# Sample tokens' y from the old states: four units' column-part products issued together

## The chip, the cores and the metric

One core of a Trainium2 chip runs the kernel in one launch. The metric is device time in microseconds (us), the median of the runs. TensorE (PE) multiplies and transposes, VectorE (DVE), ScalarE (ACT) and GpSimd (POOL) do the element work, SyncE (SP) issues the transfers.

## What is computed

The reference is one inference step of a hybrid decoder layer: a half-step SwiGLU FFN, a token mixer with a pooling branch and a Mamba-2 (SSD) branch, and a second half-step FFN. 1024 prompt tokens and 64 sample tokens (8 sequences of 8) go through it in float32. What matters here is the SSD branch of the sample tokens, which starts from given states:

```python
D_INNER = 2048; SSD_HEAD_DIM = 64; N_SSD_HEADS = 32; N_SSD_GROUPS = 4; D_STATE = 128
# state_ssm (1, 8 sequences, 32 heads, 64, 128) is h0 of the sample tokens
# exact per-token recurrence h_t = exp(dt_t A) h_{t-1} + dt_t x_t B_t^T, y_t = h_t C_t
def step(h, inp):
    s_c, d_c = inp
    return h * d_c[..., None, None] + s_c, h
h_last, h_prev = lax.scan(step, h0..., (st, chunk_decay))
y_off = jnp.einsum('bclgn,bcgrpn,bclgr->bclgrp', cr, h_prev, jnp.exp(a_cs))
y = y_diag + y_off
```

For the sample tokens there is one chunk, so `h_prev` is the old state h0: `y_off` is C times h0 times a decay, and the new state is h0 times a decay plus a sum over the eight new tokens.

## The kernel before

Activations lie with channels on the partitions, in two halves of tokens: 512 prompt tokens, then 512 prompt and the 64 sample tokens (576, in two pieces of 288). A dense projection of a 128-channel tile is a series of matmuls 128 x 128 x 288 in three products (high and low parts); `pz`, `pc` and `pso` are the PSUM tiles of such projections. Their weights come in pairs `wh`, `wl` by transfers on SP's queue, some tiles ahead.

Around this main stream run generators, called chains, which emit the small steps. `tick()` is called between the k steps of a projection; a chain's next step is emitted once an estimate `pe[0]` of PE time has passed its due time, which is the time before its last step plus what it yielded. `STEP_S` is 2.5. A scheduler then orders each engine's instructions; PE, ACT, DVE and SP each run theirs in that order.

`ssd_group` is the chain of one of four head groups. It ends, in the second half, with the sample tokens: `ssd_b` with `c == 4`. Their states are worked on in eight units, `(pr, bh)`: a pair of heads `pr` out of four, for four sequences `bh` out of two fours. A unit is one tile of 128 x 4 x 128: (head, channel) by sequence by state. For each unit the code does this:

- `load` (L1183): a transfer of the old states into `h0` (in the profile the tile is `h`), two units ahead.
- `turn` (L1188): four transposes into PSUM `ph0T`, copied by ACT into `h0T` (L1193). Before the change this is done one unit ahead.
- pyos (L1211, the helper's line is L161): for each of the four sequences, 32 columns of C against the turned state, into 32 partitions of the PSUM tile `po`, called `pyos`. Each product uses a 32-column part of the array. It is float32, two instructions each, so eight for a unit.
- pnew (L1214): one product of 96 rows by 512 columns, the new tokens' share of the state.
- DVE (L1216) forms the new state in place, and SP stores it (L1219).
- Behind the fourth pair: ACT copies `po` into `yt` (L1222), PE turns it back (`pyT`), and DVE multiplies it by the decay (L1228).

The other half of the sample tokens' y comes from `pyd` (L1237), in 64-column parts; `pfin` turns the prompt's last state. In group 0 the sample stage comes at the end of the projection `pz`, and its steps run into the next group's `pc`; in groups 1 to 3 it runs beside `pz`.

Of the kernel before, what the change touches and what calls it, by code (L numbers as in the profile page):

```python
# [14 lines left out]
P = 128  # L15
# [47 lines left out]
def tile_hybrid_pool_ssd_macaron(  # L63
# [19 lines left out]
    def nm(s):  # L83
        uid[0] += 1
        return f"{s}_{uid[0]}"

    def act(shape=(P, 576), dt=F32, name="a"):
        return sp.tile(list(shape), dt, tag="act", bufs=N_ACT, name=nm(name))
# [22 lines left out]
    def psum(tag="ps", name="ps"):  # L111
        npd = stage["npd"]
        return stage["ps"].tile([P, 512], F32, tag=tag, bufs=npd if tag == "pd" else 8 - npd, name=nm(name))
# [46 lines left out]
    def mm(out, lhsT, rhs, start=True, stop=True, free=False):  # L160
        T.matmul(out, lhsT, rhs, start=start, stop=stop, skip_group_check=free)  # L161
        pe[0] += max(out.free_size(), 64) / 2400.0 * (1 if rhs.dtype == F32R else 4)

    def tr(out, in_, idn):
        T.transpose(out, in_, idn)  # L165
        pe[0] += 0.107
# [1000 lines left out]
    def ssd_b(h, g, c, a, hold, Cf, y4, dts):  # L1167

        dt, acs, dtd, cd, cdp = dts
        abs_, xp, xd, ea, btok, L, tok = a  # L1170
        smp = c == 4
        hc = c * NH + g * HPG
        hcs = slice(hc, hc + HPG)
        ysl = y4[:, :, tok]
        first = h == 0 and c == 0
        if smp:
            units = [(pr, bh) for bh in range(2) for pr in range(4)]

            def src(u):
                gp = g * 4 + u[0]  # L1180
                return state_ssm[0, u[1] * 4 : u[1] * 4 + 4, 2 * gp : 2 * gp + 2].rearrange("b h p n -> (h p) b n")

            def load(u):  # L1183
                t = act((P, 4, P), name="h0")
                dma(t, src(u))
                return t

            def turn(h0):  # L1188
                pt = psum("ps", "ph0T")
                for b in range(4):  # L1190
                    tr(pt[:, b * P : (b + 1) * P], h0[:, b, :], ident)
                hT = act((P, 4, P), name="h0T")
                S.copy(hT.rearrange("p b n -> p (b n)"), pt)  # L1193
                return hT

            h0s = {0: load(units[0]), 1: load(units[1])}
            yield STEP_S
            hTs = {0: turn(h0s[0])}
            for i, (pr, bh) in enumerate(units):
                if i + 2 < len(units):  # L1200
                    h0s[i + 2] = load(units[i + 2])
                yield STEP_S
                if i + 1 < len(units):
                    hTs[i + 1] = turn(h0s[i + 1])
                hT, h0 = hTs.pop(i), h0s.pop(i)
                gp = g * 4 + pr


                if pr == 0:
                    po = psum("ps", "pyos")  # L1210
                for b in range(4):  # L1211
                    mm(po[b * 32 : (b + 1) * 32, pr * P : (pr + 1) * P], Cf[:, 512 + bh * 32 : 544 + bh * 32], hT[:, b, :])
                pn = psum("ps", "pnew")
                mm(pn, xd[bh][0][:, pr * P : (pr + 1) * P], xd[bh][1].rearrange("p b n -> p (b n)"))  # L1214
                for b in range(4):
                    V.scalar_tensor_tensor(h0[:, b, :], h0[:, b, :], cdp[0][:, gp, bh * 4 + b : bh * 4 + b + 1],  # L1216
                                           pn[:, b * P : (b + 1) * P], op0=ALU.mult, op1=ALU.add)
                dst = new_ssm_s[0, bh * 4 : bh * 4 + 4, 2 * gp : 2 * gp + 2].rearrange("b h p n -> (h p) b n")
                dma(dst, h0)  # L1219
                if pr == 3:  # L1220
                    yt = act((P, 512), name="yt")
                    S.copy(yt, po)  # L1222
                    pt = psum("ps", "pyT")
                    for k in range(4):
                        tr(pt[:, k * P : (k + 1) * P], yt[:, k * P : (k + 1) * P], ident)
                    own = bass.AP(pt.tensor, pt.offset, [list(pt.ap[0]), [P, 4], [40, 4], [1, NT]])
                    e = ea[:, :, bh * 32 : (bh + 1) * 32].rearrange("p q (b t) -> p q b t", t=NT)
                    V.tensor_tensor(e, own, e, op=ALU.mult)  # L1228
        elif not first:
            po = psum("ps", "pyo")  # L1230
            for pr in range(4):
                mm(po[:, pr * L : (pr + 1) * L], hold[:, pr * P : (pr + 1) * P], Cf[:, tok])
        py = psum("ps", "pyd")
        for i in range(HPG):
            m_ = abs_[i // abs_[0].shape[1]][:L, i % abs_[0].shape[1], :]
            hh = slice((i % 2) * HD, (i % 2 + 1) * HD)
            mm(py[hh, (i // 2) * L : (i // 2 + 1) * L], xp[:L, i * HD : (i + 1) * HD], m_)  # L1237
        pyv = py[:, : 4 * L].rearrange("p (q l) -> p q l", l=L)
        if first:
            V.tensor_tensor(ysl, ysl, pyv, op=ALU.add)  # L1240
        else:
            if not smp:
                V.tensor_tensor(ea, po.rearrange("p (q l) -> p q l", l=L), ea, op=ALU.mult)
            V.tensor_tensor(ea, ea, pyv, op=ALU.add)
            V.tensor_tensor(ysl, ysl, ea, op=ALU.add)
# [22 lines left out]
    def ssd_group(h, g, Bf, Cf, xs4, y4, dts):  # L1268
# [6 lines left out]
        for c in range(4 + h):  # L1275
            ga = ssd_a(h, g, c, Bf, Cf, xs4, dts)
            next(ga)
            yield step
            try:
                next(ga)  # L1280
            except StopIteration as e:
                a = e.value
            yield step
            if prev:
                for w in ssd_b(h, g, *prev, Cf, y4, dts):
                    yield w
            prev = (c, a, ssd_st(h, g, c, a, dts))
        yield step
        for w in ssd_b(h, g, *prev, Cf, y4, dts):
            yield w  # L1290
# [266 lines left out]
```

## Time and profile before

| | |
|---|---|
| time, median of 3 runs | 2952.33 us (2952.29 to 2953.47) |
| span of the profiled execution | 2950.3 us |
| instructions in the profile | 52088 |
| PE busy | 2900.3 us, 98% of the span |
| DVE / ACT / POOL busy | 1646.5 / 1187.0 / 445.1 us |
| pyos matmul instructions | 256, median 285 ns, from 1708.6 to 2056.6 us |
| ph0T transposes | 128, median 272 ns |
| pnew matmuls | 32, median 499 ns |

The span runs from the first to the last instruction of the execution that the profiler recorded; the profile gives no other time for that execution, and the times of the runs lie about 2 us above the span. [...]

### The profile page before, as it was taken

What the parts mean: (1) busy time and instruction counts of PE and PEld (TensorE: products, weight loads), DVE (VectorE), ACT (ScalarE), POOL (GpSimd) and SP (SyncE); (2) the same over time, 40 slices, a digit from 0 to 9 for tenths busy, and PEclk for the clock granted to TensorE, in tenths of its full rate; (3) what the DMA queues carried; (4) which work ended last, traced back from release to release, by engine and by line L of the source; (5) the groups of instructions that cost most, each with busy time, mean ns of one, the idle gap of its engine ahead of it and who ended that gap; (6) DMA issues with size and microseconds to landing.
All of it is one profiled execution on the core that took longest, in us unless ns stands there. A gap on an engine that the chain in (4) does not pass through costs nothing. (4 is left out here: it accounts for less than half of the span.)

```text
span 2950.3 us, 52088 instructions
## 1 busy us (share of the span) xinstructions
PE 2900.3 (98%) x19740; PEld 2689.1 (91%) x19740; DVE 1646.5 (56%) x3134; ACT 1187.0 (40%) x2418; POOL 445.1 (15%) x528
## 2 busy tenths in 40 slices
PE   7999999999999999999999999999999999999998
PEld 6999999789988888788999988999999999997898
DVE  5654445434273897777633776867665443443432
ACT  5444444333242665443332454442333433342322
POOL 5433333000000000000000010100034333330000
PEclk9999999999999999999999999999999999999999
DMA  4465554864335888678434566556574522236652
GB/s 131 155 220 176 164 161 152 271 201 142 101 98 168 276 258 265 196 225 286 118 97 152 170 184 183 168 155 186 178 240 155 165 90 76 79 106 203 197 179 72
DMA packets 542273, 501.36 MB, mean 170 GB/s; under 512 B 36388, under 2 KB 391780, under 8 KB 542014
## 3 DMA queue, kind: packets, MB, share of 16 engines
q1 hardware_dynamic: 542006, 498.03, 54.0%
q8 instruction: 155, 2.54, 0.4%
q14 instruction: 96, 0.79, 0.1%
q10 hardware_dynamic: 16, 0.00, 0.0%
HBM read 355.94 MB, written 142.20 MB: 169 GB/s over the span
## 5 line engine op out<-in xcount | busy, mean ns | idle before, releaser
L290 DVE TENSOR_TENSOR wl<-wraw,wh 128x512 fp32r<-128x512 f32 (+1 forms) x416 | 282.8, 681 | 394.7 <-ACT wh L289 386.6
L289 ACT ACTIVATE wh<-wraw 128x512 fp32r<-128x512 f32 (+1 forms) x416 | 256.4, 617 | 603.0 <-PE po L161 233.7
L161 PE MATMUL pw<-hi,wh 128*128 128x288 f32 (+1 forms) x1248 | 361.3, 289 | 2.6 <-DVE t L560 2.2
L161 PE MATMUL pw<-hi,wl 128*128 128x288 f32 (+1 forms) x1248 | 360.1, 289 | 0.0
L161 PE MATMUL pw<-lo,wh 128*128 128x288 f32 (+1 forms) x1248 | 359.9, 288 | 0.0
L161 PE MATMUL pw<-X,wh 128*128 128x288 f32 (+1 forms) x1872 | 356.9, 289 | 0.2 <-ACT t L556 0.2
L161 PEld LDWEIGHTS pw<-X,wh 128*128 128x128 f32 x1872 | 295.8, 190 | 0.4 <-ACT t L556 0.4
L161 PE MATMUL po<-hh,wh 128*128 128x288 f32 (+1 forms) x1056 | 288.1, 330 | 6.8 <-ACT hh L350 6.6
L161 PE MATMUL po<-hr,wh 128*128 128x288 f32 (+1 forms) x1056 | 289.4, 328 | 0.0
L161 PE MATMUL po<-hh,wl 128*128 128x288 f32 (+1 forms) x1056 | 288.6, 328 | 0.0
L161 PE MATMUL pw<-X,wl 128*128 128x288 f32 (+1 forms) x936 | 270.1, 289 | 0.0
L161 PEld LDWEIGHTS pw<-hi,wh 128*128 128x128 f32 x1248 | 236.2, 189 | 3.5 <-DVE t L560 2.6
L161 PEld LDWEIGHTS pw<-lo,wh 128*128 128x128 f32 x1248 | 236.1, 189 | 0.0
L161 PEld LDWEIGHTS pw<-hi,wl 128*128 128x128 f32 x1248 | 236.1, 189 | 0.0
L456 DVE TENSOR_TENSOR wl<-s,wh 128x512 fp32r<-128x512 f32 x168 | 123.4, 736 | 145.3 <-ACT wh L455 142.2
L161 PEld LDWEIGHTS po<-hh,wh 128*128 128x128 f32 x1056 | 179.0, 189 | 24.3 <-ACT hh L350 11.1
L161 PEld LDWEIGHTS po<-hr,wh 128*128 128x128 f32 x1056 | 179.9, 189 | 15.8 <-DVE hr L352 2.3
L161 PEld LDWEIGHTS po<-hh,wl 128*128 128x128 f32 x1056 | 180.0, 189 | 14.2 <-DMA wl<-part 0.4
L161 PEld LDWEIGHTS pw<-X,wl 128*128 128x128 f32 x936 | 178.1, 190 | 0.0
L455 ACT ACTIVATE wh<-s 128x512 fp32r<-128x512 f32 x168 | 106.2, 632 | 174.4 <-PE pw L161 170.7
L161 PE MATMUL pc<-hi,wh 128*128 128x288 f32 (+1 forms) x576 | 161.5, 334 | 0.0
L161 PE MATMUL pc<-lo,wh 128*128 128x288 f32 (+1 forms) x576 | 158.2, 328 | 0.0
(341 smaller groups left out, 6391.0 us busy)
## 6 DMA issues: line engine op xcount, KB each, us to landing
wh<-part SPq DMA_DIRECT2D x204, 256.0 KB
wl<-part SPq DMA_DIRECT2D x204, 256.0 KB
wraw<-in_ffn_w_in_dram SPq DMA_DIRECT2D x188, 256.0 KB
wraw<-in_w_in_dram SPq DMA_DIRECT2D x180, 256.0 KB
wraw<-in_ffn_w_out_dram SPq DMA_DIRECT2D x120, 256.0 KB
part<-wh SPq DMA_DIRECT2D x112, 256.0 KB
part<-wl SPq DMA_DIRECT2D x112, 256.0 KB
ab<-acsd SPq DMA_DIRECT2D x64, 256.0 KB
```

Of the source, the lines that this page charges most:

```text
L161: T.matmul(out, lhsT, rhs, start=start, stop=stop, skip_group_check=free)
L289: S.activation(wh, raw, AF.Copy)
L290: V.tensor_tensor(wl, raw, wh.bitcast(F32), op=ALU.subtract)
L455: S.activation(wh, a, AF.Copy)
L456: V.tensor_tensor(wl, a, wh.bitcast(F32), op=ALU.subtract)
```

## The change

The products of pyos leave their units. The turned states of four units are kept, and behind the fourth unit's pnew the sixteen products of all four are issued in a row into one PSUM tile, which is allocated only there. A unit's transposes are issued in the unit's own step, not one unit ahead. A yield of 1.0 is put between the copy of `po` and its transposes.

```diff
             h0s = {0: load(units[0]), 1: load(units[1])}
+            hTs = {}
             yield STEP_S
-            hTs = {0: turn(h0s[0])}
             for i, (pr, bh) in enumerate(units):
                 if i + 2 < len(units):
                     h0s[i + 2] = load(units[i + 2])
+                hTs[pr], h0 = turn(h0s[i]), h0s.pop(i)
                 yield STEP_S
-                if i + 1 < len(units):
-                    hTs[i + 1] = turn(h0s[i + 1])
-                hT, h0 = hTs.pop(i), h0s.pop(i)
                 gp = g * 4 + pr
-                if pr == 0:
-                    po = psum("ps", "pyos")
-                for b in range(4):
-                    mm(po[b * 32 : (b + 1) * 32, pr * P : (pr + 1) * P], Cf[:, 512 + bh * 32 : 544 + bh * 32], hT[:, b, :])
                 pn = psum("ps", "pnew")
                 mm(pn, xd[bh][0][:, pr * P : (pr + 1) * P], xd[bh][1].rearrange("p b n -> p (b n)"))
...
                 if pr == 3:
+                    po = psum("ps", "pyos")
+                    for q in range(4):
+                        for b in range(4):
+                            mm(po[b * 32 : (b + 1) * 32, q * P : (q + 1) * P], Cf[:, 512 + bh * 32 : 544 + bh * 32], hTs[q][:, b, :])
+                    hTs = {}
                     yt = act((P, 512), name="yt")
                     S.copy(yt, po)
+                    yield 1.0
                     pt = psum("ps", "pyT")
```

On PE, in head group 1, a unit stands like this before the change (each row is an instruction or a number of equal ones; the names are PSUM tile, moving or stationary operand, with their buffers' numbers):

```order
L161 MATMUL pz_20235<-hi_15086,wl_20276 128x288
L161 MATMUL pz_20236<-hi_15086,wl_20276 128x288
L165 MATMUL ph0T_20290<-ident,h_4164_20224 128x128 x4
L161 MATMUL pyos_20297<-h0T_20264,Cf_17828 32x128 x4
L161 MATMUL pnew_20302<-bblk_20098,X_4140_20091 128x512
L161 MATMUL pz_20235<-hi_15113,wh_20274 128x288
```

Twelve rows of pz follow, and the next unit. After the change the same unit stands as follows, in the same place:

```order
L161 MATMUL pz_20235<-hi_15086,wl_20276 128x288
L161 MATMUL pz_20236<-hi_15086,wl_20276 128x288
L161 MATMUL pnew_20290<-bblk_20098,X_4140_20091 128x512
L165 MATMUL ph0T_20299<-ident,h_4164_20224 128x128 x4
L161 MATMUL pz_20235<-hi_15113,wh_20274 128x288
```

The unit has lost pyos, pnew stands ahead of the next unit's transposes, and eighteen rows of pz follow. Behind the fourth unit of that group the order after the change has the products of all four:

```order
L161 MATMUL pz_20324<-hi_15113,wl_20387 128x288
L161 MATMUL pnew_20407<-bblk_20098,X_4140_20091 128x512
L161 MATMUL pyos_20414<-h0T_20266,Cf_17828 32x128 x4
L161 MATMUL pyos_20414<-h0T_20304,Cf_17828 32x128 x4
L161 MATMUL pyos_20414<-h0T_20349,Cf_17828 32x128 x4
L161 MATMUL pyos_20414<-h0T_20383,Cf_17828 32x128 x4
L161 MATMUL pz_20323<-hi_15135,wh_20385 128x288
```

Six rows of pz lie between this run and the transposes `pyT` of its result. Groups 2 and 3 and the second batch of group 0 have the same form. In the first batch of group 0, PE's rows after the change are these, behind the first two units and fourteen rows of pc:

```order
L165 MATMUL ph0T_18936<-ident,h_3924_18902 128x128 x4
L161 MATMUL pnew_18943<-bblk_18766,X_3901_18759 128x512
L165 MATMUL ph0T_18952<-ident,h_3928_18918 128x128 x4
L161 MATMUL pnew_18959<-bblk_18766,X_3901_18759 128x512
L161 MATMUL pyos_18966<-h0T_18909,Cf_17335 32x128 x4
L161 MATMUL pyos_18966<-h0T_18925,Cf_17335 32x128 x4
L161 MATMUL pyos_18966<-h0T_18941,Cf_17335 32x128 x4
L161 MATMUL pc_19114<-lo_15016,wh_19116 128x288
```

Three more rows of pc and then the fourth unit's pyos follow, so this batch is in two pieces. Outside the sample stages the order of PE differs from before only in a few places behind group 0, where `pyo`, `pyd` and some transposes of the next group's chunks stand some rows later.

## The prediction

> **What bounds the kernel now.** I read the page first, then busy time by stretches around the four places where the edited code runs, then TensorE's waits there, then the timeline inside them. The page:
>
> ```profile
> span 2950.3 us, 52088 instructions
> ...
> PE 2900.3 (98%) x19740; PEld 2689.1 (91%) x19740; DVE 1646.5 (56%) x3134; ACT 1187.0 (40%) x2418; POOL 445.1 (15%) x528
> ...
> PEclk9999999999999999999999999999999999999999
> ```
>
> TensorE (PE) is busy 98% of the span at its full granted clock; no other engine passes 56%. The busy time by stretches, one row for each of the four sample stages and, second, the stretch behind the first of them (columns: stretch, its length, then busy time of PE, PEld, DVE, ACT and POOL):
>
> ```profile
> 1707.00:1726.00 19.00, 18.44 (x181) 14.46 (x180) 10.29 (x36) 6.28 (x12) 0.19 (x1) 1.00 0.81 237
> 1726.00:1745.00 19.00, 18.32 (x136) 17.23 (x136) 15.99 (x37) 11.32 (x25) 4.96 (x10) 1.00 0.62 181
> ...
> 1812.00:1836.00 24.00, 24.00 (x225) 20.47 (x224) 11.95 (x41) 6.97 (x14) 0.19 (x1) 1.00 0.79 230
> ...
> 1930.00:1956.00 26.00, 25.85 (x227) 22.36 (x226) 11.10 (x36) 7.25 (x15) 0.00 (x0) 1.00 0.72 214
> ...
> 2036.00:2060.00 24.00, 24.00 (x225) 20.48 (x224) 12.77 (x43) 6.33 (x12) 0.00 (x0) 1.00 0.79 228
> ```
>
> Three sample stages have next to no idle PE, the first (head group 0) half a microsecond. So the time that counts is how long each instruction holds PE's in-order stream, from its start to the next start: the ends are modelled and overlap. All waits of PE from 1700 to 2100 us:
>
> ```profile
> PE pso L161 <- ACT craw L817: 1.2, 1, 1.2
> PE ph0T L165 <- DMA h<-in_state_ssm_dram: 0.7, 2, 0.5
> PE prb L161 <- POOL rsm L358: 0.7, 1, 0.7
> ```
>
> No weight load is waited for here, though the state loads and stores share SP's queue with them. One unit of group 1, from PE's timeline (start, length, instruction):
>
> ```profile
> 1818.37 0.43 PE L161 MATMUL pz<-hi,wl 128*128 128x288 f32 x2
> 1818.64 0.60 PE L165 MATMUL ph0T<-ident,h 128*128 128x128 f32 x4
> 1819.17 0.43 PE L161 MATMUL pyos<-h0T,Cf 128*32 128x128 f32 x8
> 1819.53 0.50 PE L161 MATMUL pnew<-bblk,X 96*128 96x512 f32 x1
> 1819.87 0.43 PE L161 MATMUL pz<-hi,wh 128*128 128x288 f32 x2
> ...
> 1821.46 0.60 PE L165 MATMUL ph0T<-ident,h 128*128 128x128 f32 x4
> ```
>
> The unit's own rows hold PE from 1818.64 to 1819.87, 1.23 us: four transposes 0.53, the four pyos products (two instructions each) 0.36, pnew 0.34. Twelve pz follow in 1.59, so 0.1325 each. The length of a pyos instruction hides that the eight start nearly together:
>
> ```profile
> L161 PE MATMUL pyos<-h0T,Cf x256: 272/285/298, 1708.6 to 2056.6; 128*32 128x128 f32 x128
> ```
>
> With the row's 0.43 and an instruction of 0.27 to 0.30, all eight start within about 0.15 of each other, and pnew starts some 0.2 after the last of them. That 0.2 repeats in every unit.
>
> **What a pyos group costs.** Group 0 also has places without one, and one where it stands alone between pc products:
>
> ```profile
> 1711.01 0.60 PE L165 MATMUL ph0T<-ident,h 128*128 128x128 f32 x4
> 1711.37 0.48 PE L161 MATMUL pnew<-bblk,X 96*128 96x512 f32 x1
> 1711.68 0.29 PE L161 MATMUL pc<-hi,wl 128*128 128x288 f32 x1
> ...
> 1712.52 0.52 PE L165 MATMUL ph0T<-ident,h 128*128 128x128 f32 x3 [0.54 <-DMA h<-in_state_ssm_dram]
> ...
> 1713.77 0.43 PE L161 MATMUL pc<-hi,wh 128*128 128x288 f32 x2
> 1714.13 0.42 PE L161 MATMUL pyos<-h0T,Cf 128*32 128x128 f32 x8
> 1714.49 0.53 PE L161 MATMUL pc<-lo,wh 128*128 128x288 f32 x2
> 1714.86 0.42 PE L161 MATMUL pc<-hi,wl 128*128 128x288 f32 x2
> ```
>
> Transposes and pnew without pyos between them hold PE 0.67 (1711.01 to 1711.68) against 1.23: pyos costs 0.56. Alone: 1713.77 to 1714.86 is 1.09 for four pc (4 x 0.1325 = 0.53) and the group, again 0.56. About 0.2 of it is streaming; the rest is entering the narrow shape, running dry behind it, and a late first instruction after it (pc x2 takes 0.37 there, not 0.265).
>
> **What a further group in the same run costs.** No two pyos groups are neighbours before the change. The nearest row is pyd, which uses 64-column parts, two at a time, and reuses each part eight times:
>
> ```profile
> 1702.13 1.09 PE L161 MATMUL pyd<-ab,xdt 128*64 128x128 f32 x16
> 1703.16 0.54 PE L161 MATMUL pz<-hi,wh 128*128 128x288 f32 x2
> ```
>
> and the durations of these sixteen (shortest, median, longest, ns):
>
> ```profile
> L161 PE MATMUL pyd<-ab,xdt x16: 272/272/324, 1702.1 to 1703.0; 128*64 128x128 f32 x16
> ```
>
> The last of 16 starts at 1702.13 + 1.09 - 0.27 = 1702.95; that is seven steps from pair to pair, 0.117 each, with no stop where a part gets new weights. A pyos group is two fours, so I take 2 x 0.117 = 0.23 for each further group. Bounds: 0.22, if the first step of pyd is the long one, and 0.36, if each group runs dry before the next (the pyos row itself). I take the pyd end: same 128 rows, same 128 moving columns, same mixture of reuse.
>
> The weight loads of pyos are not much shorter than that step:
>
> ```profile
> L161 PEld LDWEIGHTS pyos<-h0T,Cf x256: 106/108/110, 1708.6 to 2056.4; 128*32 128x32 f32 x128
> ```
>
> [...]
>
> **The sum.** Before, 32 groups stand in 32 runs (four head groups, eight units). After, they stand in nine: the order puts four together in seven batches, and three and one in the first batch of group 0. Joined groups: 32 - 9 = 23. Saved: 23 x (0.56 - 0.23) = 7.6 us. All of it lies on PE, which is the bound, so it counts in full. The transposes, pnew, pz, pc and all copies keep their number; DVE, ACT and POOL do the same work.
>
> Moved pieces, each with its cover:
>
> - pnew now comes out of the pz stream ahead of the transposes. Two in a row show its price:
>
> ```profile
> 1722.61 0.71 PE L161 MATMUL pnew<-bblk,X 96*128 96x512 f32 x2
> 1723.15 0.42 PE L161 MATMUL pc<-hi,wl 128*128 128x288 f32 x2
> ```
>
> 0.27 each, the late first instruction after the transposes included; in the sum it is within the 0.67 pair. I take no extra; bounds -0.04 a unit (0.27 against the 0.31 of pnew in the pair), 1.3 in all, and, as a rival, +0.41 a unit.
>
> - The first batch of group 0. The third and fourth transposes wait for state loads issued at 1707.56 to 1708.54. Before, the fourth set starts at 1712.52, where 1711.68 + 0.13 was possible: 0.7 lost. After, PE reaches it by 1707.26 (first transposes) + two pairs 1.34 + 14 pc 1.86 + one pair 0.67 = 1711.1, so it waits 1.4 for the same landing. Price +0.7; bounds 0 (an earlier landing) and +1.0.
>
> ```profile
> 1707.26 1.03 PE L165 MATMUL ph0T<-ident,h 128*128 128x128 f32 x8
> 1707.56 0.98 SPq L1185 DMA_DIRECT2D h<-in_state_ssm_dram x2
> ```
>
> - The later state loads come two units ahead of their transposes, not one, so the other 0.2 of that wait (group 2) goes: -0.2.
> - The first pyos of the fourth unit waits for the last copy of its batch by ACT:
>
> ```profile
> 1819.28 0.59 ACT L1193 COPY h0T<-ph0T 128x512 f32<-128x512 f32 x1 [1.62 <-PE ph0T L165]
> ```
>
> This copy ends 1.23 after its transposes begin. A late one would hold everything behind pyos on PE; 18 pz (2.4 us) lie between, in group 0 pnew and older groups. The wait for yt ahead of pyT has six pz or pc, 0.8 us, as cover; if ACT is late there, some tenths in eight places, at most +0.8 in all. I take zero.
> - SP: state stores wait for DVE and stand between weight loads; the unit takes 18 pz in place of 12, so the queue is less dense. Zero, since no weight load is waited for now.
> - Behind group 0 the 1.2 wait of pso for the craw copy sits in a DVE-heavy stretch, where the order puts pyo and pyd later. PE arrives earlier by group 0's share, about one microsecond. Bounds: the wait goes (-1.2) or eats that share (+1.0). Zero taken.
>
> Total: -7.6 + 0.7 - 0.2 = -7.1 us. Against the profiled execution that is a span of 2943.2. The median of the runs is 2952.33, 2.0 above the span (what lies around it, unchanged): 2945.2.
>
> **Rivals.**
>
> 1. *Each group runs dry before the next one in a run.* Then a further group costs 0.36: 23 x 0.20 = 4.6, less the 0.5 net of the other terms: 2948.2. For: before, nothing follows a pyos group within 0.2. Against: pyd.
> 2. *Weights come late for each four.* A four then takes a step and a load of the row above: 2 x (0.117 + 0.108) = 0.45, saved 23 x 0.11 = 2.5, less 0.5: 2950.3. For: the loads of pyos and its products share one stream of four parts. Against: pyd again. [...]
>
> 3. *Group 0's gain is lost behind it*, with a longer craw wait and late yt copies: 7.1 - 1.0 - 0.8 = 5.3 saved: 2947.0. For: that stretch has PE waiting for ACT and DVE already. Against: the order also moves DVE work out of its way.
> 4. *Slower: pnew's 96 rows drain the array when entered from a full stream.* Before, pnew always stands behind transposes, a pyos group or another pnew, where a drain could be hidden. If entering and leaving it cost what they do for pyos, 0.56 less its 0.15 of starts = 0.41, times 32 is 13.1: 6.0 slower, 2958.3. It decides from 0.22 a unit. Against: transposes to pnew show no gap (1711.01 to 1711.37 for four), and two pnew take 0.54.
>
> That the grouping does not happen is no rival: the order shows it, apart from the one batch split in three and one.
>
> **Chances.** The forecast's case 0.75, rivals 0.09, 0.04, 0.05 and 0.07. About 0.2% (5.9 us) is what a measurement can tell from no change, so faster means below 2946.4. Of the forecast's 0.75 I put 0.04 above that line, since 7.1 has only 1.2 to spare against waits that I set to zero: faster 0.71; same 0.04 + 0.18 = 0.22; slower 0.07. The range reaches down to 2943.1 (steps of 0.11: 23 x 0.34 = 7.8; the craw wait gone, 1.2; group 2's 0.2; no price in group 0: 9.2 saved; pnew's 1.3 is not added, as that many ends seldom meet) and up to 2948.4, past rivals 3 and 1.
>
> **What would show it.** In the changed profile a run of 32 pyos instructions should hold PE 0.56 + 3 x 0.23 = 1.25, seven times; rows of pnew and ph0T in the stream together 0.67; PE's busy time should fall by about 7 us; the wait of ph0T for its state load should be one of about 1.4 less what the modelled ends hide. A run of 1.6 means rival 1, near 1.9 rival 2; pnew followed by a gap means rival 4. The prediction is wrong if the runs take 1.25 and the time still does not fall: then PE's new slack went into waits on ACT or DVE behind group 0.

## The result

The changed kernel takes 2941.63 us (median, 2940.19 to 2943.37) against 2952.31 (2948.60 to 2953.47) for the kernel before in the same comparison, six runs each: a ratio of 0.9969 on record, 95% interval 0.9959 to 0.9979 (it is not the quotient of the two medians, which is 0.9964). It is faster by more than 0.2%, as forecast; the median lies 1.5 us below the low end of the predicted range (2943.1, which is 0.9969 of the 2952.33 that the prediction started from). In two further comparisons, beside 26 runs each of the kernel before, the difference was 8.4 and 8.0 us (2942.00 against 2950.36, ratio 0.9975 [0.9966, 0.9984]; 2942.14 against 2950.15, ratio 0.9972 [0.9962, 0.9981]). Predicted were 7.1.

The head of the page of the changed kernel:

```profile
span 2939.7 us, 52093 instructions
...
PE 2891.4 (98%) x19740; PEld 2688.6 (91%) x19740; DVE 1644.6 (56%) x3134; ACT 1186.9 (40%) x2418; POOL 445.3 (15%) x528
```

The span fell by 10.6 us and PE's busy time by 8.9; no other engine moved by more than 2. The end of the first batch of group 1, from PE's timeline, and a unit of it:

```profile
1810.67 0.40 PE L161 MATMUL pnew<-bblk,X 96*128 96x512 f32 x1
1810.90 0.60 PE L165 MATMUL ph0T<-ident,h 128*128 128x128 f32 x4
1811.26 0.50 PE L161 MATMUL pz<-hi,wh 128*128 128x288 f32 x2
1811.60 0.42 PE L161 MATMUL pz<-lo,wh 128*128 128x288 f32 x2
...
1819.83 0.40 PE L161 MATMUL pnew<-bblk,X 96*128 96x512 f32 x1
1820.16 1.08 PE L161 MATMUL pyos<-h0T,Cf 128*32 128x128 f32 x32
1821.17 0.53 PE L161 MATMUL pz<-hi,wh 128*128 128x288 f32 x2
1821.54 0.43 PE L161 MATMUL pz<-lo,wh 128*128 128x288 f32 x2
```

The 32 pyos hold PE from 1820.16 to 1821.17, 1.01. Around them, pnew's step is 0.33 and not 0.23, and the next two pz take 0.37 and not 0.265 (two of the prediction's 0.1325): 0.10 and 0.105 more. Together 1.22; predicted 1.25. pnew and the transposes without pyos hold 0.23 + 0.36, and the late pz behind them 0.08: 0.67, as predicted. There is no gap behind pnew, so rival 4 is out.

**Where the time went.** One product, `pcb` with 64 columns, is issued once at the start of each group's sample work, and `pss` on 64 rows ends the part behind group 3. Their starts cut the program into stretches. Before, from PE's timeline (start, length, instruction):

```profile
1695.65 0.33 PE L161 MATMUL pcb<-Cf,Bf 128*64 128x64 f32 x2
1795.96 0.33 PE L161 MATMUL pcb<-Cf,Bf 128*64 128x64 f32 x2
1918.66 0.33 PE L161 MATMUL pcb<-Cf,Bf 128*64 128x64 f32 x2
2019.86 0.33 PE L161 MATMUL pcb<-Cf,Bf 128*64 128x64 f32 x2
2087.56 0.43 PE L161 MATMUL pss<-ident,rsm 64*128 64x64 f32 x2
```

and in the changed kernel:

```profile
1696.14 0.33 PE L161 MATMUL pcb<-Cf,Bf 128*64 128x64 f32 x2
1793.83 0.33 PE L161 MATMUL pcb<-Cf,Bf 128*64 128x64 f32 x2
1914.20 0.33 PE L161 MATMUL pcb<-Cf,Bf 128*64 128x64 f32 x2
2013.00 0.33 PE L161 MATMUL pcb<-Cf,Bf 128*64 128x64 f32 x2
2079.28 0.43 PE L161 MATMUL pss<-ident,rsm 64*128 64x64 f32 x2
```

The distances between these rows, and from the last one to the end of the span, for every execution profiled in this study (us; the kernels are those of the experiments below):

| kernel | joins | group 0 | group 1 | group 2 | group 3 | behind |
|---|---|---|---|---|---|---|
| before | 0 | 100.31 | 122.70 | 101.20 | 67.70 | 862.74 |
| before, again | 0 | 100.17 | 123.15 | 101.06 | 67.95 | 861.72 |
| changed | 23 | 97.69 | 120.37 | 98.80 | 66.28 | 860.42 |
| changed, again | 23 | 98.84 | 120.37 | 98.80 | 66.26 | 859.81 |
| changed, third | 23 | 99.05 | 120.37 | 98.79 | 65.58 | 859.95 |
| apart | 0 | 99.40 | 122.42 | 100.80 | 68.30 | 860.23 |
| pairs | 12 | 98.07 | 120.97 | 99.40 | 66.87 | 859.93 |
| eight | 28 | 99.50 | 120.08 | 98.51 | 65.90 | 860.13 |
| eight, again | 28 | 99.56 | 120.09 | 98.51 | 65.98 | 858.81 |
| ahead | 24 | 99.84 | 120.44 | 98.87 | 66.33 | 860.85 |
| twice | 23 | 100.36 | 122.12 | 100.54 | 68.06 | 860.03 |
| group 0 old | 18 | 100.09 | 120.38 | 98.80 | 66.30 | 860.68 |
| group 0 only | 5 | 97.63 | 122.56 | 101.12 | 68.46 | 859.90 |

From before to changed, group 0 gives 2.62, group 1 2.33, group 2 2.40, group 3 1.42: 8.77 in the edited part. Another 2.32 lies behind it, where the edit changes nothing, and 0.49 is lost ahead of it. The table is the instrument of all that follows: in groups 1 and 2 it repeats to 0.01 between executions of the changed kernel. Each row is one execution, and a wait that another lacks shows in full. In "before, again" group 1 is 0.45 longer, by a wait of PE for a state load:

```profile
1827.42 0.63 PE L165 MATMUL ph0T<-ident,h 128*128 128x128 f32 x4 [0.47 <-DMA h<-in_state_ssm_dram]
```

The first profile of before has none there, but 0.15 of it in group 2. Without these two waits the stretches of groups 1 and 2 agree to 0.02.

### The profile page after: what moved, and what is told of

The parts are those of the page before. It is cut to its first block, busy times and chain, and to the rows that moved or that the text cites. A ratio compares the mean times of both kernels' runs of the same rounds, so it can differ in the third digit from the quotient of the medians.

```text
span 2939.7 us, 52093 instructions
## 1 busy us (share of the span) xinstructions
PE 2891.4 (98%) x19740; PEld 2688.6 (91%) x19740; DVE 1644.6 (56%) x3134; ACT 1186.9 (40%) x2418; POOL 445.3 (15%) x528
## 4 chain that ended last, share of the span: by engine, by line
PE 93%; DMA 2%; DVE 2%; ACT 1%; issue 1%; SPq 0%; POOL 0%; POOLq 0%; ACTq 0%; DVEq 0%
PE pw L161 28%; PE po L161 17%; PE pc L161 9%; PE pg L161 8%; PE pz L161 7%; PE pso L161 5%; PE pu L161 5%; PE pwo L161 3%; PE pbp L161 3%; DMA hr<-hd 1%; PE pyd L161 1%; PE pst L161 1%; PE pyo L161 1%; PE pgm L161 1%; PE ptx L161 0%
## 5 line engine op out<-in xcount | busy, mean ns | idle before, releaser
L161 PEld LDWEIGHTS po<-hh,wh 128*128 128x128 f32 x1056 | 178.8, 188 | 23.9 <-ACT hh L350 10.6
L161 PE MATMUL pc<-hi,wl 128*128 128x288 f32 (+1 forms) x576 | 158.2, 328 | 0.0
```

## Experiments

**Theories.** *Joins*: a pyos group costs 0.56 alone and 0.23 as a further one of a run, so each join gives 0.33. Rivals: each group still runs dry (0.20 a join), or the weights come late (0.11 a join), and the rest of the gain comes from the transposes and pnew having moved, or from the part behind group 0. Every edit below is against the changed kernel.

**The moves without the joins (apart).** Transposes in the unit's own step, as in the changed kernel; the products of each unit stay by themselves.

```diff
                 gp = g * 4 + pr
+                if pr == 0:
+                    po = psum("ps", "pyos")
+                for b in range(4):
+                    mm(po[b * 32 : (b + 1) * 32, pr * P : (pr + 1) * P], Cf[:, 512 + bh * 32 : 544 + bh * 32], hTs[pr][:, b, :])
                 pn = psum("ps", "pnew")
...
                 if pr == 3:
-                    po = psum("ps", "pyos")
-                    for q in range(4):
-                        for b in range(4):
-                            mm(po[b * 32 : (b + 1) * 32, q * P : (q + 1) * P], Cf[:, 512 + bh * 32 : 544 + bh * 32], hTs[q][:, b, :])
-                    hTs = {}
```

> Undoes the grouping alone: the transposes stay in the unit's own step as after the change, but each unit's four products are issued in the unit again, so pyos stands in 32 runs. Theory (joined groups save 0.34 us each, since a run of four holds PE 1.22 us with its edges and four single groups 4 x 0.56): no join, so the time is that of before, 2951 to 2953 us. Rival (the gain comes from moving the transposes and the state loads' lead): 2941 to 2943 us, as after the change.

Measured: 2947.05 us (2944.50 to 2949.88) against 2951.07, ratio 0.9989 [0.9981, 0.9998]. This is 4.0 less than before, more than the theory had. By the table: 0.91 in group 0, 0.28 in group 1, 0.40 in group 2, 0.6 more in group 3, and 2.5 less behind the edited part. Most of the miss is not from the edited code's own rows. What is: 0.28 and 0.40, of which the gone state wait is 0.15 in group 2. The prediction's bound of -0.04 a unit for the moved pnew would be 0.3 a group; it had been left at zero. In PE's timeline of this kernel, a unit reads:

```profile
1814.33 0.42 PE L161 MATMUL pz<-hi,wl 128*128 128x288 f32 x2
1814.68 0.43 PE L161 MATMUL pyos<-h0T,Cf 128*32 128x128 f32 x8
1815.04 0.50 PE L161 MATMUL pnew<-bblk,X 96*128 96x512 f32 x1
1815.38 0.60 PE L165 MATMUL ph0T<-ident,h 128*128 128x128 f32 x4
1815.73 0.50 PE L161 MATMUL pz<-hi,wh 128*128 128x288 f32 x2
1816.07 0.42 PE L161 MATMUL pz<-lo,wh 128*128 128x288 f32 x2
1816.33 0.43 PE L161 MATMUL pz<-hi,wl 128*128 128x288 f32 x2
```

From 1814.33 to 1816.33 is 2.00, less six pz (0.795): the unit holds 1.205, where before it held 1.235. The new order of its parts is worth 0.03 a unit.

Against this kernel the changed one differs by the joins alone: 2.05, 2.00 and 2.02 in groups 1, 2 and 3, for six joins each. That is 0.333 to 0.342 a join. For all 23 joins this makes 7.7. The medians would leave the joins less, the 8.0 to 8.4 of the whole change less the 4.0 of this kernel, but they are too coarse to decide: the interval of this kernel's ratio alone spans 0.6 to 5.6 us.

**Runs of two (pairs).** Products behind every second unit.

```diff
-                if pr == 3:
+                if pr % 2:
...
-                    for q in range(4):
+                    for q in (pr - 1, pr):
...
```

> Half the grouping: products are issued in twos, behind the second and the fourth unit. The order has 12 joined groups in groups 1 to 3 and none in group 0. Theory: 12 x 0.34 = 4.1 us less than before, about 2948.2 us; a run of two holds PE from its first start to the next instruction 0.36 + 0.22 = 0.58 us. Rival (the transposes' move): 2941 to 2943 us.

Measured: 2944.11 us (2942.41 to 2948.12) against 2951.07, ratio 0.9979 [0.9970, 0.9987]. Four joins a group stand 1.45 and 1.40 below "apart" in groups 1 and 2: 0.36 and 0.35 each. A run of two holds PE 0.58 (1814.44 to 1815.02), as expected. The time as a whole is 4 below the expected one, by the stretch behind and by group 0. Group 0 is not as in "apart": it is 2.24 below before without one join, and PE waits there neither for craw nor for rsm, 1.2 and 0.7 before. So group 0's stretch can't be read as joins.

**Runs of eight units (eight).** All products of a group behind its eighth unit, two copies `yt` behind them.

```diff
-                hTs[pr], h0 = turn(h0s[i]), h0s.pop(i)
+                hTs[i], h0 = turn(h0s[i]), h0s.pop(i)
...
-                if pr == 3:
+                if i == 7:
+                    for bq in range(2):
...
```

> All eight units of a head group in one run, in two PSUM tiles: four runs, 28 joined groups, five more than after the change. Theory: 28 x 0.34 = 9.5 us less than before; 5 x 0.34 = 1.7 us less than after the change, about 2940 us; a run holds PE 1.01 + 4 x 0.22 = 1.89 us. If late copies of the result or of the last state hold PE: as after the change or up to 2 us more.

Measured: 2942.07 us (2940.33 to 2944.46) against 2951.07, ratio 0.9972 [0.9961, 0.9982]. That is 2 above the expected 2940, within what was expected if late copies hold PE. A run holds PE 1.89 (1832.64 to 1834.53), as expected, and one further join in each of groups 1 and 2 gives 0.29 in each, but group 0's stretch is longer than the changed kernel's by 0.45 to 1.81 us, for all its joins.

**Grouping alone (ahead).** The products as in the changed kernel, the transposes one unit ahead as before.

```diff
-            hTs = {}
             yield STEP_S
+            hTs = {0: turn(h0s[0])}
...
-                hTs[pr], h0 = turn(h0s[i]), h0s.pop(i)
                 yield STEP_S
+                if i + 1 < len(units):
+                    hTs[i + 1] = turn(h0s[i + 1])
+                h0 = h0s.pop(i)
...
```

> The grouping alone: behind the fourth unit as after the change, but the transposes one unit ahead as before it. The order has eight runs of four, also in the first batch of group 0: 24 joined groups. Theory: 8.2 us less than before and 0.3 less than after the change, 2941 to 2944 us. Rival (the transposes' move carries the gain): 2950 to 2953 us.

Measured: 2944.57 us (2941.80 to 2947.38) against 2951.07, ratio 0.9981 [0.9972, 0.9990]. This is 0.6 above the expected range and clear of the rival's. Groups 1 and 2 are within 0.07 of the changed kernel's; group 0 is only 0.47 below before, with 1.8 of waiting for state loads and 1.1 for rsm (0.5 and 0.7 before). The grouping carries the gain in groups 1 to 3; where the transposes stand hardly matters there.

**Both kernels again, and eight again.** "Apart" and "pairs" had come out about 4 us below what the joins alone would make them, and "eight" 2 above it, so the two kernels and "eight" ran once more, without an edit.

> The kernel before once more, for a second profile of it. Theory (a part of the difference between the first two profiles lies outside the edited code: at the start of the second FFN's output products PE waits for a hidden tile, and in the first profile of before the granted clock was 0.66 from 2666 to 2671 us behind that wait): the second profile has a wait of that place too, of 1.0 to 2.0 us, and where it is under 1.5 the clock stays at 1.00 and the span is about 2 us shorter, 2947 to 2949 us; the sample stages take the same time as before within 0.3 us. Rival (the edit itself shortens that place): the clock falls again and the span is 2950 us.

> The changed kernel once more, beside the others of this call on one chip. Theory (23 joined groups at 0.34 us, 7.9, and about 1 us in and behind group 0): 8 to 10 us less than before on this chip. Rival (10.7 as first measured is all of it the edit): 10.7 us less.

> All eight units in one run, once more, beside the changed kernel on the same chip. Theory: five more joined groups, 1.7 us less than the changed kernel. Rival (the longer wait for the last copies gives it back): the same as the changed kernel within 0.5 us.

Measured: before, one run, 2951.84; changed 2942.00 (2940.57 to 2945.85); eight 2942.72 (2941.05 to 2945.08), ratio 0.9974 [0.9965, 0.9983], all against 2950.36. The changed kernel is 8.4 below before, as expected. The second profile of before has the expected wait (1.1) and the clock at 1.00, but its span is 2950.1 where 2947 to 2949 was expected, and its group 1 is 0.45 longer where at most 0.3 was. "Eight" does gain 0.28, 0.29 and 0.28 over the changed kernel of the same chip in groups 1 to 3, but loses 0.72 in group 0, so that the whole is no faster. PE's waits of 1690 to 1800 us in "eight, again":

```profile
PE ph0T L165 <- DMA h<-in_state_ssm_dram: 1.5, 3, 1.1
PE pso L161 <- ACT craw L817: 1.2, 1, 1.2
PE prb L161 <- POOL rsm L358: 1.1, 1, 1.1
```

In the changed kernel PE waits 0.9 for pso, for another ACT row, and 0.2 for rsm there. Those two differences are 1.2, against two further joins in group 0. Longer runs than four units give back in group 0 what they win elsewhere.

**Every run twice (twice).** Each run's products are issued a second time, with the same operands into the same tile, so a run is 64 instructions and its edges are unchanged: what it adds is eight groups of streaming in a head group and nothing else.

```diff
-                    for q in range(4):
+                    for q in (0, 1, 2, 3, 0, 1, 2, 3):
```

> The changed kernel with every product of a run issued twice, so that runs hold 64 instructions; the second pass writes the same values over the first. It measures the step itself. Theory (a further group of four products costs 0.22 us in a run): 32 x 0.22 = 7.0 us more than the changed kernel; a run of 64 holds PE 1.01 + 0.87 = 1.88 us. Rival (weights come late for each four, 0.45 a group): 14.4 us more; rival (each group runs dry, 0.36): 11.5 us more.

Measured: 2948.93 us (2944.68 to 2952.84), 6.9 above the changed kernel on the same chip. Groups 1, 2 and 3 are 1.75, 1.74 and 1.80 longer: 0.22 for each further pyos group. A run in PE's timeline:

```profile
1823.25 0.40 PE L161 MATMUL pnew<-bblk,X 96*128 96x512 f32 x1
1823.58 1.96 PE L161 MATMUL pyos<-h0T,Cf 128*32 128x128 f32 x64
1825.46 0.53 PE L161 MATMUL pz<-hi,wh 128*128 128x288 f32 x2
1825.83 0.43 PE L161 MATMUL pz<-lo,wh 128*128 128x288 f32 x2
```

64 instructions hold 1.88, where 32 held 1.01: 0.87 for four more groups, 0.22 each, with the same 0.37 behind. Rival 1 (0.36) and rival 2 (0.45) are both out.

**The two halves.** "Group 0 old" gives group 0 the code of before and the rest that of the change, one behind the other in two branches; in "group 0 only" the first line reads `g > 0`.

```diff
+            if g == 0:
+                h0s = {0: load(units[0]), 1: load(units[1])}
+                yield STEP_S
+                hTs = {0: turn(h0s[0])}
+                for i, (pr, bh) in enumerate(units):
...
+            else:
+                h0s = {0: load(units[0]), 1: load(units[1])}
+                hTs = {}
+                yield STEP_S
+                for i, (pr, bh) in enumerate(units):
...
```

> Head group 0 in the order of before, head groups 1 to 3 in that of the change: 18 joins. By the sum (0.33 a join, group 2's wait gone) 6.2 below before, about 2944.2; if each join saved only 0.2, 2946.6. If the part of the saving that the sum missed comes from head group 0 and the stretch behind it, this kernel shows none of it and stands at 6.2; if it comes from the joins themselves (over 0.4 each) it stands 7.5 or more below.

> Only head group 0 in the order of the change: 5 joins. By the sum 1.65 saved less 0.7 for the state load's wait: about 0.95 below before, 2949.4. If the wait costs nothing more than before and the order itself helps behind group 0, 2 to 3 below, about 2947.9. If the gain is lost behind the group, no change.

> The changed kernel once more, beside the two halves of it: if the halves add up, it stands below before by what they save together; the wait for the third state load in its profile is either near 0.4 or near 1.4, as in the two profiles so far.

Measured against 2950.15: group 0 old 2943.39 us (2941.25 to 2945.43), ratio 0.9976 [0.9967, 0.9985], 6.8 less; group 0 only 2949.17 (2944.55 to 2952.17), ratio 0.9996 [0.9988, 1.0005], 1.0 less; the changed kernel 2942.14, 8.0 less. The halves add up to 7.7. Expected were 6.2 and 0.95 for the two halves. The profile of "group 0 only" shows a larger gain in group 0 than its median does, 2.68, with 0.4 of waiting for a state load, the low one of the values that the next section shows. That execution is the fastest of its eleven runs, 4.6 below their median; it reaches the first `pcb` at 1693.03, 2.6 sooner than before, where the edit changes nothing.

## Why the prediction held, and where it missed

**What a join is worth: right.** 0.33 predicted, 0.333 to 0.342 by six joins in each of three groups, 0.22 for a further group where 0.23 was taken. Taking pyd as the nearest row was the right choice. No run shows a load and a product one behind the other, as rival 2 priced them with 0.45 a group: the loads of the run of 32 shown above, 0.106 to 0.110 each, lie in 0.81 us beside its products, from the timeline of the weight loads:

```profile
1820.16 0.81 PEld L161 LDWEIGHTS pyos<-h0T,Cf 128*32 128x32 f32 x32 [0.27 <-issue]
```

**Moved pieces: mis-sized.** Zero was taken, with a bound of -0.04 a unit; "apart" shows -0.03 in its rows and -0.28 in group 1's stretch. The stretch is less sure than the row: "group 0 only", in the order of before there, has 122.56 in group 1, 0.14 above "apart". 32 units at 0.03 are about 1 us, an estimate, and the larger part of what the sum lacks.

**The first batch of group 0: the price +0.7 is not one number.** The prediction had 1.4 for the wait. PE's transposes in the changed kernel's first profile:

```profile
1707.76 0.60 PE L165 MATMUL ph0T<-ident,h 128*128 128x128 f32 x4
1708.44 0.60 PE L165 MATMUL ph0T<-ident,h 128*128 128x128 f32 x4
1711.54 0.63 PE L165 MATMUL ph0T<-ident,h 128*128 128x128 f32 x4 [0.40 <-DMA h<-in_state_ssm_dram]
1712.43 0.63 PE L165 MATMUL ph0T<-ident,h 128*128 128x128 f32 x4
```

and in the second:

```profile
1707.34 0.60 PE L165 MATMUL ph0T<-ident,h 128*128 128x128 f32 x4
1708.02 0.60 PE L165 MATMUL ph0T<-ident,h 128*128 128x128 f32 x4
1710.90 0.63 PE L165 MATMUL ph0T<-ident,h 128*128 128x128 f32 x4 [0.18 <-DMA h<-in_state_ssm_dram]
1713.13 0.63 PE L165 MATMUL ph0T<-ident,h 128*128 128x128 f32 x4 [1.37 <-DMA h<-in_state_ssm_dram]
```

The same program waits 0.40 once and 1.55 the other time (the third profile: 0.32 and 1.47), by when the state load lands, and group 0's stretch follows: 97.69, 98.84, 99.05. Two of three executions have the predicted wait; the first, on which the first span rests, has the lower bound, and that is luck. SP's queue issues these loads 0.30 behind PE's first transposes in all three, so the difference lies behind the issue; why the load lands a microsecond apart is not shown.

**Behind the groups: the waits moved.** All waits of PE from 1700 to 2100 us in the changed kernel's first profile:

```profile
PE prb L161 <- POOL rsm L358: 0.9, 2, 0.7
PE pso L161 <- ACT acc L1342: 0.9, 1, 0.9
PE ph0T L165 <- DMA h<-in_state_ssm_dram: 0.4, 1, 0.4
```

The 1.2 for craw became 0.9 for another ACT row, and prb behind group 0 waits 0.23 in place of 0.68: 0.75 gained, where zero had been taken inside bounds of -1.2 and +1.0. Against that a wait that no step had named appeared at the end of group 3:

```profile
2078.19 1.16 PE L161 MATMUL prb<-ident,rsm 128*128 128x128 f32 x8 [0.70 <-POOL rsm L358]
```

It is there in "apart" too, without joins, and not in the third profile of the changed kernel. The two nearly cancel. Rival 3 is out: group 0's gain was not lost. That the waits moved the right way was not foreseen either; in "ahead" and in "eight" the wait for rsm grew to 1.1.

**The sum again.** In the first profile: joins 23 x 0.335 = 7.7, moved pieces 1.0, group 2's wait 0.15, group 0's waits 0.75 + 0.1, less 0.7 at the end of group 3: 9.0, against 8.77 in the stretches. With the later landing it is 7.9, against 7.64 in the second profile (384.27 in place of 391.91 from the first `pcb` to `pss`). The whole is 8.4 and 8.0 in the two later comparisons.

**What remains of the first comparison's 10.7.** 2.3 lies behind the edited part. There the first profile of before has a wait in the second FFN that runs on into slow matmuls:

```profile
2664.65 0.40 PE L161 MATMUL po<-hh,wl 128*128 128x512 f32 x1
2666.89 0.80 PE L161 MATMUL po<-hh,wh 128*128 128x512 f32 x2 [1.84 <-ACT hh L350]
...
2669.49 0.63 PE L161 MATMUL po<-hh,wh 128*128 128x512 f32 x1
2669.92 0.63 PE L161 MATMUL po<-hr,wh 128*128 128x512 f32 x1
...
2671.27 0.39 PE L161 MATMUL po<-hh,wl 128*128 128x512 f32 x1
2671.50 0.39 PE L161 MATMUL po<-hh,wh 128*128 128x512 f32 x1
```

The steps between single matmuls are mostly 0.43 there and 0.23 behind them. PE's busy time, instructions and granted clock in that stretch (columns as in the prediction's table of stretches):

```profile
2666.00:2671.00 5.00, 4.11 (x10) 3.03 (x11) 2.04 (x3) 1.89 (x3) 0.00 (x0) 0.66 0.95 318
```

The same wait by PE, from its waits between 2640 and 2720 us (total, times, longest). In the profile of before, and then in the second one of the same kernel:

```profile
PE po L161 <- ACT hh L350: 3.5, 3, 1.8
```

```profile
PE po L161 <- ACT hh L350: 2.5, 3, 1.1
```

In the changed kernel's first profile and in its second:

```profile
PE po L161 <- ACT hh L350: 2.8, 3, 1.4
```

```profile
PE po L161 <- ACT hh L350: 1.5, 3, 0.6
```

The stretch behind the 1.4 of the changed kernel, as the one above:

```profile
2657.50:2662.50 5.00, 4.13 (x17) 3.09 (x18) 1.63 (x3) 1.89 (x3) 0.00 (x0) 1.00 0.97 347
```

The wait varies by 1 us between executions of one kernel. From 2655 to 2710 us the granted clock is below 1.00 in the first profile of before alone, 0.74 from 2665 to 2670; it is 1.00 in the second, in the first two of the changed kernel, in both of "eight" and in "apart", "pairs" and "ahead". So the order of before does not bring it by itself, and "apart", without a join, has 860.23 behind the edited part like the others. Both executions of before are longer there (862.74 and 861.72) than all eleven of the other kernels (858.81 to 860.85). Most of this lies in one stretch that holds these waits, from the first `pw` behind that `pss` to the first `ptf`: 484.4 in the first profile of before, 482.8 in the second, 480.6 to 482.4 in the eleven others. Of the second's surplus another 0.6 stands ahead of that stretch, as 0.7 does in "changed, third". So the second execution of before is 0.4 beyond what the other kernels show there, and the first, with its slow matmuls, 2.0. What makes these waits scatter stays open. The other part is the median that the prediction started from: 2952.33 from three runs, where 81 runs of before, in three later comparisons, have medians of 2950.15 to 2951.07. From 2950.3 the sum of 7.1 would have given 2943.2, 1.1 above what the changed kernel takes there, which is about the estimate for the moved pieces.

## What to carry to other kernels

A small product on a part of the array can cost mostly its edges: here 0.34 of 0.56 us is paid once a run, whether the run has one, two, four or eight groups. Look for such products that stand alone in a stream of another shape, let them wait until several are ready, and stop where the next one delays a consumer: four units won, eight won no more. Sum a change from stretches between instructions that occur once, not from the span: in groups 1 and 2 the stretches of the changed kernel repeated to 0.01 us, where the medians of before moved by 2. Look into a stretch for waits before subtracting it: group 0's moved by 1.4 in one program, with a state load.

## What the runs showed of the hardware

- Products on 32-column parts that share all 128 rows took 0.87 us for 32 more instructions of a run, 0.11 for each four, where one weight load alone takes 0.106 to 0.110.
- The instruction ahead of a run takes 0.10 more and the two behind it 0.105 more. With 0.22 a group, 0.13 remains of the 1.01 that a run of four groups holds PE; where in the run it falls is not shown.
- In one execution a wait of 1.84 us was followed by about 4 us at steps of mostly 0.43, with 0.23 ahead of the wait and behind them, the granted clock 0.66 in the mean of the 5 us around it; a wait of 1.4 in the changed kernel was not: the clock is 1.00 there and the steps are 0.23 from the fourth matmul on. Whether the length of the wait decides is not shown.
- One program waited 0.40, 1.55 and 1.79 us for the same state loads of 256 KB in three executions, at the same distance behind their issue.
